# Router product on un-normalised rows, a reordered output projection, and an earlier start for three regions of the weight ring

## The chip, the cores and the metric

The kernel runs on one core of a Trainium2 chip. The core has five engines that matter here: TensorE (PE), VectorE (DVE), ScalarE (ACT), GpSimd (POOL) and SyncE (SP), whose queue issues the transfers from HBM. The metric is the device time of one execution in microseconds; the median of three runs of the kernel before is 1281.34 us (1281.11 to 1286.21).

## The reference, in short

One block of 256 tokens by 1024 channels, in fp32:

```python
u = _modulate(x, sh1, sc1)                      # layer norm, scale and shift
mix = _mixer(u, w_in, ...)                      # attention, gated linear attention, merge, w_out
x = _post_norm(ALPHA * x + (1 + g1) * mix, ln1_g, ln1_b)
u = _modulate(x, sh2, sc2)
ffn = _moe(u, w_router, b_router, w_up, b_up, w_down, b_down)
x = _post_norm(ALPHA * x + (1 + g2) * ffn, ln2_g, ln2_b)
```

The mixer projects u by w_in to 8 heads of forgetting attention, 4 heads of gated linear attention (GLA) and two gates. Each branch goes through a weight of its own, the two are merged by sigmoid gates, and w_out (1024 by 1024) projects the sum. `_moe` takes 32 logits per token from the normalised and modulated rows, keeps the four largest, takes a softmax over them, and adds up the outputs of those four experts, each a clamped SwiGLU with w_up (1024 by 2048) and w_down (1024 by 1024).

## The kernel before

The kernel is written as tasks, Python generators, that issue instructions to the five engines. The main line issues TensorE's large products, and between them `Tasks.tick` (line 346) lets the small tasks (GLA, attention, the vector work of the norms) put in theirs. When a task's turn comes is decided while the program is built, by a model of time, `Pace`: `Pace.cost` (line 95) gives each instruction a cost, and a task that yields a time waits until the modelled PE has come that far. The order on each engine is thus fixed in the program. All instructions pass through one helper, so every row has line 209, and rows are told apart by their tiles.

Weights stream from HBM through `Ring` (line 224). It holds regions of 1 MB by name; GV and KB, U1 and U2, LQ and FA, GS and GX are mates that lie side by side, shown as one tile of 2 MB (GVKB, U1U, LQFA, GSGX). A load is issued on SP's queue as soon as the program has a free region for it, in the order in which loads were asked for, and SP waits there until the last reader of that region is done. What stands behind it in SP's queue waits too.

The stages are these. The modulation vector and the input projection come first, with attention and GLA woven in (0 to about 304 us together with the branch products). Weights of the projections are split into two parts that TensorE multiplies in three passes: `split` (line 675) copies the high part on ACT and subtracts on DVE or POOL. The splits go into buffers of the pool `pair`: once GLA is done (`after_gla`, line 1329) the regions named in PAIR join it. `ada_task` (line 875) makes the columns of the modulation vector, `gate_mul` (line 1464) multiplies a branch by its gate and writes QA, and `merge` (line 1469) adds the branches. Then follow the output projection, eight half-loads of w_out (slots j) by two token blocks, in the order of the table ORDER, into the banks pz; `z_task` (line 1576) for each token block (z = alpha x + gated mixer output, layer norm, its transposes, the router product by `wr`, which `router_task` folds the modulation into, the four largest, one-hot rows W); and the gather, in which TensorE multiplies one-hot rows with the normalised rows (QA at that time). The loop over experts then runs `up_proj`, the activation and `down` for 32 experts, eight MB of w_up and four of w_down each. HALVES at the top gives the loads of the first experts as single regions.

In the tile names below, W_72, W_73, W_2713 are buffers of one pool; b_63 to b_70 are PSUM banks; x in rows of the order counts equal instructions in a row.

## Time and profile before

| | |
|---|---|
| median of three runs | 1281.34 us |
| profiled execution | 1283.55 us |
| its span | 1281.4 us |
| PE busy | 1177.7 us (92%) |
| DVE, ACT, POOL busy | 488.5, 262.0, 90.9 us |
| read from HBM | 469.43 MB, 367 GB/s over the span |

The table by stage below has one line for each stretch of the span. Its columns are the stretch, its length, the busy time and the instructions of PE, of PE's weight loads, of DVE, ACT and POOL, then the granted clock of TensorE as a share of full speed, the DMA share and the rate in GB/s. In the timelines each row is a group of neighbouring instructions of one kind: start in us, busy time, engine, line, operation, output<-input, shapes, count, and in brackets the idle time ahead of it with what ended it. SPq rows are issues of transfers, and their time includes waiting for the region.

### The profile page before, as it was taken

The numbers are of one execution on the slowest core, as the hardware profiler recorded it, in microseconds if no ns is written. First come the engines' busy times: TensorE is split into PE (matmuls) and PEld (weight loads), VectorE is DVE, ScalarE is ACT, GpSimd is POOL, SyncE is SP. The second block draws the span as 40 slices with busy tenths as digits, with TensorE's granted clock in tenths as the row PEclk, the third lists the DMA queues.
The fourth block names the chain that finished last, engine by engine and source line by source line (L and its number), as shares of the span: only waits on it lengthen the run. The fifth ranks groups of instructions, "written<-read, shape, count | busy, mean of one in ns | idle before, by whom it ended". The sixth has DMA issues, their size and how long they took to land. (4 is left out here: it accounts for less than half of the span.)

```text
span 1281.4 us, 15734 instructions
## 1 busy us (share of the span) xinstructions
PE 1177.7 (92%) x6478; PEld 603.9 (47%) x6478; DVE 488.5 (38%) x1053; ACT 262.0 (20%) x518; POOL 90.9 (7%) x61
## 2 busy tenths in 40 slices
PE   6999999989699999999989899898989898988995
PEld 4797677788534344343433334242434333333432
DVE  5645764457523224323333222322232332322233
ACT  3355544452211111010110101010101011010101
POOL 3412421020100000000000000000000000000000
PEclk9999999999799999999999999999999999999998
DMA  9953446895899999999999999999999999999994
GB/s 306 313 168 119 179 140 247 329 327 198 338 377 429 420 430 426 430 427 426 430 426 427 429 427 429 427 426 430 427 427 429 427 428 428 425 429 428 428 412 156
DMA packets 73061, 471.55 MB, mean 368 GB/s; under 512 B 7581, under 2 KB 28093, under 8 KB 45978
## 3 DMA queue, kind: packets, MB, share of 16 engines
q1 hardware_dynamic: 72794, 470.23, 90.2%
q8 instruction: 53, 0.87, 0.3%
q10 hardware_dynamic: 192, 0.27, 0.1%
q14 instruction: 22, 0.18, 0.0%
HBM read 469.43 MB, written 1.05 MB: 367 GB/s over the span
## 5 line engine op out<-in xcount | busy, mean ns | idle before, releaser
L209 PE MATMUL b<-U1U,W 128*128 128x256 f32 (+1 forms) x840 | 142.6, 410 | 11.0 <-DMA U1U<-in_w_down_dram 8.7
L209 DVE COPY W<-b 128x512 f32<-128x512 f32 x32 | 22.1, 691 | 296.8 <-PE b L209 296.8
L209 PEld LDWEIGHTS b<-U1U,W 128*128 128x128 f32 (+1 forms) x840 | 86.7, 169 | 67.1 <-issue 58.7
L209 DVE TENSOR_TENSOR W<-b,SP 128x512 f32<-128x512 f32 (+1 forms) x33 | 22.3, 675 | 221.1 <-PE b L209 221.1
L209 DVE TENSOR_TENSOR GL<-b,GL 128x512 f32<-128x512 f32 x124 | 76.9, 682 | 53.8 <-PE b L209 53.8
L209 PE MATMUL b<-YB1NB,W 128*64 128x512 f32 (+2 forms) x416 | 86.2, 542 | 4.5 <-DVE SP L209 4.0
L209 PE MATMUL b<-YAW,W 128*64 128x512 f32 (+1 forms) x384 | 82.3, 555 | 6.3 <-DVE SP L209 5.3
L209 PE MATMUL b<-R2YB,W 128*64 128x512 f32 x344 | 78.2, 595 | 9.1 <-DMA R2YB<-in_w_down_dram 7.2
L209 PE MATMUL b<-GSGX,W 128*64 128x512 f32 x336 | 76.2, 594 | 11.0 <-DMA GSGX<-in_w_down_dram 8.6
L209 PE MATMUL b<-R0R,W 128*64 128x512 f32 (+1 forms) x368 | 80.2, 578 | 4.6 <-DMA R0R<-in_w_up_dram 4.1
L209 PE MATMUL b<-GVKB,W 128*64 128x512 f32 x336 | 78.1, 608 | 5.0 <-DMA GVKB<-in_w_up_dram 5.0
L209 PE MATMUL b<-LQFA,W 128*64 128x512 f32 x336 | 77.8, 606 | 4.1 <-DMA LQFA<-in_w_up_dram 4.1
L209 ACT ACTIVATE W<-b 128x512 f32<-128x512 f32 x32 | 19.1, 597 | 303.3 <-PE b L209 303.3
L209 PE MATMUL b<-ADAM,W 128*64 128x512 f32 x336 | 75.9, 593 | 4.2 <-DVE SP L209 4.0
L209 ACT ACTIVATE SP<-b 128x256 f32<-128x256 f32 (+1 forms) x34 | 12.8, 378 | 309.3 <-PE b L209 309.3
L209 PEld LDWEIGHTS b<-W,QA 128*128 128x128 f32 x512 | 63.9, 203 | 13.9 <-DVE GL L209 11.4
L209 POOL TENSOR_TENSOR GL<-GL,QB 128x512 f32<-128x512 f32 x2 | 2.9, 1427 | 942.8 <-ACT GL L209 942.7
L209 PE MATMUL b<-W,QA 128*128 128x128 f32 x512 | 67.3, 291 | 0.6 <-DVE W L209 0.6
L209 PE MATMUL b<-W,SP 64*128 64x512 f32 (+1 forms) x264 | 63.9, 602 | 0.5 <-DVE W L209 0.5
L209 ACT ACTIVATE W<-b,scol 128x128 f32<-128x128 f32 x124 | 46.9, 457 | 64.4 <-PE b L209 60.0
L209 PEld LDWEIGHTS b<-YB1NB,W 128*64 128x64 f32 (+1 forms) x416 | 32.8, 143 | 55.4 <-issue 46.0
L209 PEld LDWEIGHTS b<-YAW,W 128*64 128x64 f32 (+1 forms) x384 | 30.8, 144 | 55.1 <-issue 44.6
(329 smaller groups left out, 1400.2 us busy)
## 6 DMA issues: line engine op xcount, KB each, us to landing
GVKB<-in_w_up_dram SPq DMA_DIRECT2D x21, 2048.0 KB
R0R<-in_w_up_dram SPq DMA_DIRECT2D x20, 2048.0 KB
LQFA<-in_w_up_dram SPq DMA_DIRECT2D x20, 2048.0 KB
YB1NB<-in_w_up_dram SPq DMA_DIRECT2D x11, 2048.0 KB
U1U<-in_w_up_dram SPq DMA_DIRECT2D x11, 2048.0 KB
YAW<-in_w_up_dram SPq DMA_DIRECT2D x11, 2048.0 KB
GSGX<-in_w_up_dram SPq DMA_DIRECT2D x11, 2048.0 KB
YAW<-in_w_down_dram SPq DMA_DIRECT2D x10, 2048.0 KB
```

What stands on the lines that cost most here:

```text
L209: r = f(*a, **k)
```

## The change

The layer norm behind the output projection is taken out of the router product. With r the inverse deviation and m the mean of a row, the normalised row is r (z - m) g + b, and the product with the router weights is linear in z: `weigh` folds g and b into the weights (two matmuls with a matrix of ones), keeps the constant row in `c1row`, and the raw z is transposed and multiplied at once by a new task, `zT_task`. `z_task` applies r, c1row, and the second norm's inverse deviation to the 32 logits. For token block 0 the sums for mean and variance come from accumulating outputs on DVE and a Square on ACT (`squares`), for block 1 from bn_stats as before. The normalising of block 0 leaves POOL. w_out is loaded by column halves, and ORDER runs the first column half for both token blocks, the second for block 0, then for block 1. PAIR keeps GV and KB; U1 and U2 go to the ring when GLA is done, and LQ is no longer called back. The count and gate matmuls go behind expert 0's up product. Two small loads of ln1's g and b as columns are new, and three constants of `Pace.cost` change, which moves the order of all tasks in the front.

```diff
-                return (n if n > m else 4 * m) / 2400.0 if a[1].dtype == F32R else n / 2400.0
+                return (n if n > m else 4 * m) / 2400.0 + 0.0135 if a[1].dtype == F32R else n / 1200.0
...
-                return n / 4200.0
+                return n / 2200.0
...
-        r = half_loads(w_out[0, (q // 2) * 512:], 4, (q % 2) * 512)[0]
+        r = half_loads(w_out[0, (q % 2) * 512:], 4, (q // 2) * 512)[0]
...
+    gbcol = small("gbcol", [128, 2, KC])
...
+        for i, r in enumerate((ln1_g, ln1_b)):
+            SP.dma_start(gbcol[:, i].rearrange("p (i j) -> p i j", j=UPJ),
+                         r[0].rearrange("(i p j) -> p i j", p=128, j=UPJ))
...
-            ring.recall(*ONCE)
+            ring.recall(*ONCE[:-1])
...
-    zx, ln1, ztb, late = [], [], [], []
+    both("U1")
+    ring.add("U1", "U2")
+    zx, ln1, late = [], [], []
...
-        DVE.tensor_tensor(tmp, wr, scol[:, 0, :, None].to_broadcast([128, KC, E]), op=OP.mult)
+
+        def weigh(shift, scale, row):
+            DVE.tensor_tensor(tmp, wr, shift[:, :, None].to_broadcast([128, KC, E]), op=OP.mult)
+            DVE.tensor_tensor(wr, wr, scale[:, :, None].to_broadcast([128, KC, E]), op=OP.mult)
+            yield
+            p = yield from aux.get()
+            for i, t in enumerate((tmp, wr)):
+                PE.matmul(p[:, i * 256:(i + 1) * 256], ones, t.rearrange(FLAT), start=True, stop=True)
+            yield
+            for i, d in enumerate((row, cs)):
+                DVE.tensor_reduce(d, p[:, i * 256:(i + 1) * 256].rearrange("p (k e) -> p e k", k=KC), axis=AX.X,
+                                  op=OP.add)
+            aux.put(p)
+            DVE.scalar_tensor_tensor(wr, cs[:, None, :].to_broadcast([128, KC, E]), -1.0 / D, wr,
+                                     op0=OP.mult, op1=OP.add)
...
+        yield from weigh(scol[:, 0], scol[:, 1], tmp[:, 0, :])
...
+        yield from weigh(gbcol[:, 1], gbcol[:, 0], c1row)
...
+
+    def zT_task(tb):
+
...
+            while f"z{tb}{n}" not in side.flags:
...
-        if tb:
-            ring.add("FA")
-        mv = mean_var(st)
-        end = pace.at["DVE"] + 0.15
-        u = u2[tb]
-        for n in range(2):
-            s = slice(n * 512, (n + 1) * 512)
-            yield end if n else pace.when(z[:, s]) - 0.85
+            yield pace.when(z[:, n * 512:(n + 1) * 512]) - 0.85
             p = yield from mm.get()
...
+            side.flags.add(f"zT{tb}{n}")
             ACT.activation(x1T[:, n * 4:n * 4 + 4, tb * 128:(tb + 1) * 128],
                            p.rearrange("p (a b) -> p a b", a=4), AF.Copy)
             mm.put(p)
...
+    def squares(z, tmp, sums):
+
+        mv = per.tile([128, 4], F32, tag="mv", bufs=6, name="mv")
+        DVE.tensor_scalar(mv[:, 0:1], sums[:, 0:1], sums[:, 1:2], 1.0 / D, op0=OP.add, op1=OP.mult)
+        DVE.tensor_scalar(sums[:, 2:3], mv[:, 0:1], -1.0, None, op0=OP.mult)
+        ACT.activation(tmp, z, AF.Square, bias=sums[:, 2:3], accum_out=sums[:, 3:4])
+        ACT.activation(mv[:, 1:2], sums[:, 3:4], AF.Copy, scale=1.0 / D)
+        return mv
...
+        for n in range(2):
+            while f"pz{tb}{n}" not in side.flags:
+                yield
+            s, zt = slice(n * 512, (n + 1) * 512), u[:, 0:512]
+            DVE.tensor_tensor(zt, pz[tb][n], g1row[:, s], op=OP.mult)
+            mm.put(pz[tb][n])
+            if tb:
+                DVE.scalar_tensor_tensor(z[:, s], z[:, s], ALPHA, zt, op0=OP.mult, op1=OP.add)
+                DVE.bn_stats(st[:, n, :], z[:, s])
+            else:
+                DVE.scalar_tensor_tensor(z[:, s], z[:, s], ALPHA, zt, op0=OP.mult, op1=OP.add,
+                                         accum_out=sums[:, n:n + 1])
+            side.flags.add(f"z{tb}{n}")
+            if n:
+                mv = mean_var(st) if tb else squares(z, u, sums)
+                rstd(mv)
+            yield
+        while not all(f"zT{tb}{n}" in side.flags for n in range(2)):
...
+        h = [z[:, i * 512:(i + 1) * 512] for i in range(2)]
+        if tb:
+            st = bn_tile()
+        DVE.scalar_tensor_tensor(h[0], h[0], mv[:, 0:1], ln1[0], op0=OP.subtract, op1=OP.mult)
+        DVE.scalar_tensor_tensor(mv[:, 3:4], mv[:, 0:1], -1.0, mv[:, 2:3], op0=OP.mult, op1=OP.mult)
+        if tb:
+            DVE.scalar_tensor_tensor(h[0], h[0], mv[:, 2:3], ln1[2], op0=OP.mult, op1=OP.add)
+        else:
+            sums = ss_tile()
+            DVE.scalar_tensor_tensor(h[0], h[0], mv[:, 2:3], ln1[2], op0=OP.mult, op1=OP.add, accum_out=sums[:, 0:1])
+        ACT.activation(h[1], h[1], AF.Identity, bias=mv[:, 3:4], scale=mv[:, 2:3])
+        yield
+        DVE.tensor_tensor(h[1], h[1], ln1[1], op=OP.mult)
+        if tb:
+            DVE.tensor_tensor(h[1], h[1], ln1[3], op=OP.add)
+            for n in range(2):
+                DVE.bn_stats(st[:, n, :], h[n])
+            ring.add("FA")
+            m1 = mean_var(st)
...
+            DVE.scalar_tensor_tensor(h[1], h[1], 1.0, ln1[3], op0=OP.mult, op1=OP.add, accum_out=sums[:, 1:2])
+        while f"raw{tb}" not in side.flags:
+            yield
+        if not tb:
+            m1 = squares(z, u, sums)
+        rstd(m1)
+        if not tb:
+            yield pace.at["ACT"] - 0.3
+        while f"raw{tb}" not in side.flags:
+            yield
+        p = V.raw[tb]
+        DVE.scalar_tensor_tensor(lg[:, 0:E], p[:, 256:256 + E], mv[:, 2:3], c1row, op0=OP.mult, op1=OP.add)
+        DVE.scalar_tensor_tensor(lg[:, 0:E], lg[:, 0:E], m1[:, 2:3], brow, op0=OP.mult, op1=OP.add)
+        mm.put(p)
         DVE.max(t8, lg[:, 0:E])
-        DVE.tensor_scalar(nm[:, 0:1], t8[:, 0:1], -1.0, None, op0=OP.mult)
         DVE.memset(t8[:, 4:8], NEG)
         DVE.match_replace(l2, t8, lg, TAKEN)
         DVE.tensor_tensor(msk[:, tb, :], l2[:, 0:E], lg[:, 0:E], op=OP.not_equal)
+        DVE.scalar_tensor_tensor(m1[:, 3:4], m1[:, 0:1], -1.0, m1[:, 2:3], op0=OP.mult, op1=OP.mult)
...
+        ACT.activation(u, z, AF.Identity, bias=m1[:, 3:4], scale=m1[:, 2:3])
...
+        yield pace.when(msk[:, tb, :]) - 0.85
...
-        s, n, k0 = NB_ + j, j // 2 % 2, j // 4 * 4 + j % 2 * 2
+        s, n, k0 = NB_ + j, j // 4, j % 4 * 2
         preps(s, AHEAD)
         mm_N([pz[0][n], pz[1][n]], parts[s], k0, m_of, KC, tbs)
         if 1 in tbs:
-            t = parts[s][2]
             used(s)
-            if s + AHEAD >= NO and Bufs.key(t) in where:
-                pair.free.remove(t)
-                ring.add(where[Bufs.key(t)])
+            if s == NO - 1 or NO - 1 in parts:
+                for t in [t for t in pair.free if Bufs.key(t) in where]:
+                    pair.free.remove(t)
+                    ring.add(where[Bufs.key(t)])
...
-    for tb in range(2):
-        PE.matmul(cnt[0:1, 0:E], onesb[:, 0:1], msk[:, tb, :], start=(tb == 0), stop=(tb == 1))
...
-    for tb in range(2):
-        for n in range(2):
-            PE.matmul(gt_p[64 * n:64 * n + E, tb * 128:(tb + 1) * 128], gates[:, tb, :], ident, start=True, stop=True)
...
+                PE.matmul(cnt[0:1, 0:E], onesb[:, 0:1], msk[:, tb, :], start=(tb == 0), stop=(tb == 1))
+                for n in range(2):
+                    PE.matmul(gt_p[64 * n:64 * n + E, tb * 128:(tb + 1) * 128], gates[:, tb, :], ident,
+                              start=True, stop=True)
...
-ORDER = [(T0, 0), (T0, 1), (T0, 2), (T0, 3), (T1, 0), (T1, 1), (T0, 4), (T0, 5), (T0, 6), (T0, 7),
-         (T1, 4), (T1, 5), (T1, 2), (T1, 3), (T1, 6), (T1, 7)]
+ORDER = [((0, 1), j) for j in range(4)] + [(T0, j) for j in range(4, 8)] + [(T1, j) for j in range(4, 8)]
...
-PAIR = ("U1", "U2", "GV", "KB")
+PAIR = ("GV", "KB")
```

The instructions on DVE around the first branch's gate product (QA<-QA,b_63). Rows with a weight region, W_.., YAW_.., GVKB or U1U_71 as output and the same tile as input are the subtraction of a split. Before:

```order
L209 TENSOR_TENSOR U1U_71<-LQFA,U1U_71 128x1024 x2
L209 TENSOR_TENSOR GVKB<-LQFA,GVKB 128x1024
L209 TENSOR_TENSOR GVKB<-R2YB_103,GVKB 128x1024
L209 TENSOR_TENSOR W_73<-R2YB_103,W_73 128x1024
L209 TENSOR_TENSOR YAW_606<-R2YB_103,YAW_606 128x1024
L209 TENSOR_TENSOR QA<-QA,b_63 128x512
L209 TENSOR_TENSOR QA<-QA,b_64 128x512
```

and after:

```order
L209 TENSOR_TENSOR W_72<-R0R_107,W_72 128x1024
L209 TENSOR_TENSOR GVKB<-R0R_107,GVKB 128x1024
L209 TENSOR_TENSOR GVKB<-ADAM,GVKB 128x1024
L209 TENSOR_TENSOR W_73<-ADAM,W_73 128x1024
L209 TENSOR_TENSOR YAW_607<-R2YB_103,YAW_607 128x1024
L209 TENSOR_TENSOR QA<-QA,b_63 128x512
L209 TENSOR_TENSOR QA<-QA,b_64 128x512
```

U1U_71 no longer takes splits, and the splits between the last branch weights and the gate product are other ones, from R0R_107 and ADAM.

The transfers that SP issues behind the ada columns (in_w_ada) into GSGX, whose region GLA frees. Before, from there on:

```order
L209 DMA R2YB_103<-in_w_in_dram 128x4x512
L209 DMA R0R_107<-in_w_in_dram 128x4x512
L209 DMA GSGX<-in_w_ada_dram 128x2048 x2
L209 DMA GL<-in_w_branch_a_dram 128x4x512
L209 DMA LQFA<-in_w_branch_a_dram 128x4x512
L209 DMA LQFA<-in_w_branch_b_dram 128x4x512
```

and after:

```order
L209 DMA ADAM<-in_w_in_dram 128x4x512
L209 DMA R2YB_103<-in_w_in_dram 128x4x512
L209 DMA GSGX<-in_w_ada_dram 128x2048 x2
L209 DMA GL<-in_w_in_dram 128x4x512
L209 DMA LQFA<-in_w_in_dram 128x4x512
L209 DMA LQFA<-in_w_ada_dram 128x2048
L209 DMA R2YB_103<-in_w_ada_dram 128x2048
L209 DMA R0R_107<-in_w_branch_a_dram 128x4x512 x2
```

Two loads of w_in now stand behind the two into GSGX, in GL and LQFA; all of w_in stood ahead of them before.

TensorE from the last rounds of the output projection (GSGX as the right operand) on. Transposes are products of ident and GL, the router product is QB with wr, the product with stack sums its partial results, the gather is W with QA. Before:

```order
L209 MATMUL b_66<-U1U_71,GSGX 128x512 x6
L209 MATMUL b_66<-GVKB,GSGX 128x512 x6
L209 MATMUL b_63<-ident,GL 128x128 x4
L209 MATMUL b_64<-ident,GL 128x128 x4
L209 MATMUL b_65<-QB,wr 32x128 x8
L209 MATMUL b_65<-stack,SP 128x32
L209 MATMUL b_66<-ident,GL 128x128 x4
L209 MATMUL b_63<-ident,GL 128x128 x4
L209 LDWEIGHTS strict
L209 MATMUL b_64<-msk,strict 128x32
L209 MATMUL b_66<-QB,wr 32x128 x8
L209 MATMUL b_67<-W_2713,QA 128x128 x4
```

and after:

```order
L209 MATMUL b_63<-ident,GL 128x128 x4
L209 MATMUL b_64<-GVKB,GSGX 128x512 x6
L209 MATMUL b_65<-ident,GL 128x128 x4
L209 MATMUL b_66<-YAW_607,GSGX 128x512 x6
L209 MATMUL b_66<-W_72,GSGX 128x512 x3
L209 MATMUL b_63<-ident,GL 128x128 x4
L209 MATMUL b_66<-W_72,GSGX 128x512 x3
L209 MATMUL b_66<-GVKB,GSGX 128x512 x12
L209 MATMUL b_64<-QB,wr 32x128 x8
L209 MATMUL b_65<-ident,GL 128x128 x4
L209 MATMUL b_64<-stack,SP 128x32
L209 MATMUL b_63<-QB,wr 32x128 x8
```

Three of the four groups of transposes moved into the output projection, and both router products now stand ahead of the first mask's product with strict.

## Rows read from the trace of the kernel before

**Rows 1.** By stage: the columns named above, core 0.
```profile
222.00:258.60 36.60, 34.63 (x272) 28.51 (x271) 14.14 (x16) 15.55 (x19) 4.09 (x2) 0.95 0.91 337
258.60:304.50 45.90, 41.62 (x310) 38.99 (x309) 29.44 (x38) 22.16 (x26) 9.45 (x5) 0.96 0.68 240
304.50:326.50 22.00, 22.00 (x98) 17.89 (x97) 12.99 (x20) 5.29 (x8) 2.50 (x4) 1.00 0.65 233
326.50:351.80 25.30, 15.40 (x98) 11.03 (x97) 15.45 (x48) 6.80 (x19) 4.18 (x3) 0.66 0.97 408
351.80:375.80 24.00, 23.09 (x102) 8.30 (x102) 7.97 (x21) 4.53 (x7) 0.00 (x0) 0.93 0.96 390
375.80:1243.00 867.20, 807.92 (x3950) 325.98 (x3948) 267.03 (x633) 100.12 (x244) 0.00 (x0) 1.00 1.01 427
```

**Rows 2.** Timeline of SP's queue.
```profile
217.43 1.15 SPq L209 DMA_DIRECT2D R0R<-in_w_in_dram  x2
...
238.74 0.97 SPq L209 DMA_DIRECT2D GSGX<-in_w_ada_dram  x2
...
328.31 8.18 SPq L209 DMA_DIRECT2D LQFA<-in_w_up_dram  x2
...
375.78 0.33 SPq L209 DMA_DIRECT2D GVKB<-in_w_up_dram  x1
```

**Rows 3.** PE's timeline in expert 0, and stretches of 1.7 us.
```profile
370.39 5.35 PE L209 MATMUL b<-GVKB,W 128*64 128x512 f32 x16
375.57 3.60 PE L209 MATMUL b<-YAW,W 128*64 128x512 f32 x16
...
341.80:343.50 1.70, 1.70 (x11) 1.70 (x11) 0.00 (x0) 0.00 (x0) 0.00 (x0) 0.59 1.02 434
370.70:372.40 1.70, 1.70 (x6) 0.49 (x4) 1.70 (x4) 0.00 (x0) 0.00 (x0) 0.50 1.02 434
374.10:375.80 1.70, 1.70 (x10) 0.58 (x8) 1.60 (x5) 0.42 (x1) 0.00 (x0) 1.00 0.36 154
```

**Rows 4.** PE's timeline in the last part of the input projection.
```profile
225.91 0.51 PE L209 MATMUL b<-U1U,YAW 128*128 128x256 f32 x2 [1.22 <-ACT YAW L209]
...
231.26 1.10 PE L209 MATMUL b<-ident,LQFA 128*128 128x128 f32 x8
...
240.10 3.04 PE L209 MATMUL b<-U1U,YAW 128*128 128x256 f32 x24
```

**Rows 5.** DVE and PE in the branch stage.
```profile
270.66 3.38 DVE L209 TENSOR_TENSOR YAW<-R2YB,YAW 128x1024 fp32r<-128x1024 f32 x1
...
274.79 1.49 PE L209 MATMUL b<-YB1NB,U1U 128*128 128x256 f32 x6 [3.89 <-DVE QA L209]
...
287.61 0.59 PE L209 MATMUL b<-gT,ones 128*128 128x256 f32 x2
```

**Rows 6.** PE, a group of four transposes in the branch stage.
```profile
278.21 0.69 PE L209 MATMUL b<-ident,ADAM 128*128 128x128 f32 x4
```

**Rows 7.** Timeline of all engines from there to expert 0.
```profile
301.81 1.06 ACT L209 ACTIVATE U1U<-R2YB 128x1024 fp32r<-128x1024 f32 x1
...
325.10 5.66 POOL L209 TENSOR_TENSOR GL<-GL,LQFA 128x512 f32<-128x512 f32 x4 [19.42 <-issue]
326.54 0.69 DVE L209 TENSOR_TENSOR LQFA<-b,ADAM 128x512 f32<-128x512 f32 x1 [2.43 <-PE b L209]
...
333.05 3.05 DVE L209 SCALAR_TENSOR_TENSOR GL<-GL,mv,LQFA 128x512 f32<-128x512 f32 x4
...
340.50 3.34 PE L209 MATMUL b<-W,QA 128*128 128x128 f32 x16
...
344.03 0.25 DVE L209 SCALAR_TENSOR_TENSOR lg<-b,mv,brow 128x32 f32<-128x32 f32 x1 [3.21 <-PE b L209]
...
346.07 3.38 PE L209 MATMUL b<-W,QA 128*128 128x128 f32 x16 [0.60 <-DVE W L209]
...
351.47 0.41 PE L209 MATMUL b<-ident,gates 128*32 128x128 f32 x4 [1.43 <-DVE gates L209]
```

More of the change, by code (lines that the diff above doesn't have):

```diff
@@ L1389, in again_task @@
             SP.dma_start(t, rows(r, D))
-        while ring.busy("LQ"):
-            yield
-        own("LQ")
-        ztb.extend(cut("LQ", 512, 0, 2))
         side.flags.add("again")
@@ L1560, in slots_out @@
                 DVE.tensor_scalar(d, q, scol[:, 1, k:k + 1], scol[:, 0, k:k + 1], op0=OP.mult, op1=OP.add)
[L1562 to L1565 removed]
+    V.raw = {}
+    def zT_task(tb):
+        z = zx[tb]
         for n in range(2):
[L1567 to L1609 removed]
+            while f"z{tb}{n}" not in side.flags:
+                yield
+            yield pace.when(z[:, n * 512:(n + 1) * 512]) - 0.85
             p = yield from mm.get()
@@ L1633, in z_task, with ss_tile @@
         PE.matmul(p[:, 256:256 + E], lT, stack, start=True, stop=True)
-        yield
+        V.raw[tb] = p
+        side.flags.add(f"raw{tb}")
+    def ss_tile():
+        return per.tile([128, 6], F32, tag="ss", bufs=3, name="ss")
+    def squares(z, tmp, sums):
[5 more added lines that the diff above has]
+        return mv
+    def z_task(tb):
+        while not ("g1" in side.flags and "again" in side.flags):
+            yield
+        z, u, st, sums = zx[tb], u2[tb], bn_tile(), ss_tile()
         lg, l2, ex = [small(f"{n}{tb}", [128, E + 4]) for n in ("lg", "l2", "ex")]
@@ L1637, in z_task @@
         DVE.memset(lg[:, E:E + 4], NEG)
-        DVE.scalar_tensor_tensor(lg[:, 0:E], p[:, 256:256 + E], mv[:, 2:3], brow, op0=OP.mult, op1=OP.add)
+        for n in range(2):
[15 more added lines that the diff above has]
+            yield
@@ L1659, in z_task @@
                 px.append((yield from aux.get()))
-            yield pace.when(u[:, 512 * i:512 * i + 512]) - 0.8
+            yield pace.when(u) - 0.8
             while tb and f"half{i}" not in side.flags:
@@ L1668, in z_task @@
                 aux.put(px[i])
+        side.flags.add(f"placed{tb}")
         DVE.scalar_tensor_tensor(ex[:, 0:E], ex[:, 0:E], 1.0, msk[:, tb, :], op0=OP.mult, op1=OP.mult,
@@ L1677, in block_kernel @@
     side.add(z_task(1))
+    side.add(zT_task(0), "again")
+    side.add(zT_task(1), "again")
     order = ORDER
     for tbs, j in order:
[L1680 removed]
+        s, n, k0 = NB_ + j, j // 4, j % 4 * 2
         preps(s, AHEAD)
@@ L1706, in block_kernel @@
     gT = small("gT", [128, T])
-    for tb in range(2):
-        for n in range(2):
-            PE.matmul(gt_p[64 * n:64 * n + E, tb * 128:(tb + 1) * 128], gates[:, tb, :], ident, start=True, stop=True)
     ACT.preload_act_table(AF.Sigmoid)
@@ L1976, in block_kernel @@
             for tb in range(2):
+                PE.matmul(cnt[0:1, 0:E], onesb[:, 0:1], msk[:, tb, :], start=(tb == 0), stop=(tb == 1))
+                for n in range(2):
+                    PE.matmul(gt_p[64 * n:64 * n + E, tb * 128:(tb + 1) * 128], gates[:, tb, :], ident,
+                              start=True, stop=True)
+            for tb in range(2):
                 ACT.activation(zx[tb], zx[tb], AF.Copy, scale=ALPHA)
```

62 lines of the change are left out of this document (8 added, 54 removed).

## The prediction

> **What bounds the kernel now.** I read the busy time by stage first, then what SP issues where two stages meet, then the stages' operations in order of time. From 375.8 to 1243 us the weight transfer is full: DMA share 1.01, 427 GB/s, while TensorE is busy 808 of 867 us [rows 1]. Nothing in the diff changes the bytes or the loop over experts, so that stretch can only shift. What decides when it starts is one queue entry: SP issues the load into region GVKB at 375.78 [rows 2], when TensorE has read expert 0's weights out of it (sixteen matmuls from 370.39, 5.35 us [rows 3]). In 374.1 to 375.8 the DMA share is 0.36: the early loads have run out and the transfers wait for this issue [rows 3]. So at this point the kernel waits for TensorE, not for memory. TensorE starts expert 0 at 351.8 and GVKB is free 24.0 later, so the end of the run stands at a fixed distance behind the start of the experts, T = 351.8, as long as the early loads last. The stages before T are TensorE's: 34.63 busy of 36.60, 41.62 of 45.90, 22.00 of 22.00 [rows 1]. Only the last, 326.5 to 351.8, is a chain across engines: TensorE is busy 15.40 of 25.30 with a granted clock of 0.66 [rows 1]. I therefore add up what each part does to T. Letters: I is the end of the input projection (258.6), S and E the start and end of the output projection (304.5, 326.5); a prime marks the new time.
>
> **Input projection, to I.** TensorE is idle for 36.60 − 34.63 = 1.97 us here, of which 1.22 stand ahead of 225.91, for a split weight [rows 4]; its load was issued at 217.43 [rows 2], because no region was free sooner. After, GLA's last transposes stand some 15 us of TensorE work earlier in the order, so GSGX, GL and LQFA come free earlier and take loads. I take half, −1.0; ends −2.0 (all of it) and, if the new order makes stalls of its own, the +6 of the last rival.
>
> **Branches, I to S.** The 45.9 hold 4.3 of idle. The large piece is 3.89 ahead of 274.79: TensorE waits for DVE's product of gate and branch [rows 5]. That product stood behind weight splits on DVE, one of them 3.38 us long at 270.66 [rows 5]. PAIR now holds two regions, not four, so five buffers are free for splits, not seven, and DVE runs fewer of them ahead: after, the product is done about 11.1 us behind I', and the bank is wanted 13.6 behind it. Cost of the same stage: the second call of weigh adds two matmuls over wr and gT; the pair before takes 0.59 [rows 5], so with the second operand's pair about +1.0 in all. −4.3 + 1.0 = −3.3. Ends: −4.3 (the pair lies in a gap) and +1.0 (another split blocks the product). The two column loads of gbcol go out near 80 us, where DMA is mostly idle; I cost them at nothing.
>
> **Output projection, S to E.** The twelve rounds keep their matmuls: 22.0. Three of the four groups of z's transposes now lie inside, four matmuls each, 0.69 by the row at 278.21 [rows 6]: +2.1. Both token blocks go together for the first four column-halves, so block 0's first half is complete early and its transposes and its normalising lie beside the last rounds. The splits that come later because of two buffers fewer have 2 to 3 us of slack by my walk through the order, so no stall is added. Ends 0 and +4 (one late split).
>
> **Tail, E to T, 25.3 before.** What goes: POOL's four passes over block 0, 5.66 us from 325.10, for which TensorE's transposes waited [rows 7]; and the count and gate matmuls ahead of T, 349.4 to 351.8, 2.3 us, their last waiting 1.43 for the gates [rows 7]. They move behind expert 0's up product. What comes, in time behind E', at the durations of the same forms: z's last half by 1.5 (0.69 each, as at 326.54 [rows 7]), its statistics by 2.45; on DVE, second half of block 0 normalised by 3.95, first of block 1 by 5.55, second by 7.4 (four such passes took 3.05 at 333.05 [rows 7]), statistics by 9.0. Block 0's logits to mask take 1.4 more, 10.45 (the like chain before begins at 344.03 and its one-hot releases the gather at 346.07 [rows 7]), small ones 10.75. Then ACT normalises block 0 for the gather, 1.06 for 128x1024 [rows 7], and the inverse deviation of block 1 is queued behind that: 12.6. Block 1's mask 13.8, block 0's one-hot 14.65. Block 0's gather is sixteen matmuls; the two before took 3.34 and 3.38 [rows 7], at a granted clock of 0.59 in the row that I have for the first [rows 3]. TensorE waits before it, as it did then, so 3.4: 18.1. Block 1's follows with no break: 1.7 if the clock is up by then, 3.4 if not; between, and closer to the first, since in the down product the clock rose from 0.50 to 1.00 while TensorE worked on [rows 3]: T' = E' + 20.2. 20.2 − 25.3 = −5.1. Ends: 18.0 (both gathers at 1.7) and 25.3.
>
> The Trainium skill ("TensorE: Matmul & The Clock Gate", section on why it matters for your kernels) says that idle gaps between bursts of matmuls drop the engine to half rate. The wait of several us ahead of the gathers is such a gap, and the trace agrees: 0.50 to 0.59 behind waits. If that speaks for both gathers, T' is E' + 21.4; I hold it as a case.
>
> **Behind T.** The count and gate matmuls and their copies, about 2.3 at the rate of before, less the wait: +0.5, since expert 0 waits for the activation there anyway. Ends −1.75 (the sixteen matmuls of 370.39 took 5.35 at clock 0.50, those of 375.57 3.60 [rows 3]; if TensorE stops less, the difference is won) and +1.0.
>
> **Whether transfers last.** Before, two loads into LQFA at 328.31 held SP's queue for 8.18 us, waiting on their region [rows 2]. After, U1U and LQFA take 3 MB before E', 7.3 us at 427 GB/s, in a stretch whose DMA share is 0.65 to 0.68 [rows 1]. From E' about 9 MB, 22 us, are left; they are done near S' + 65, GVKB's issue on TensorE's path is due at S' + 24.05 + 20.2 + 24.5 = S' + 68.7. TensorE's path still decides, by 3.6. Without the 3 MB the transfer would end near S' + 72.4 and take its place.
>
> **Sum.** −1.0 − 3.3 + 2.1 − 5.1 + 0.5 = −6.8 against the profiled execution's 1283.55 (its span is 1281.4): 1276.75. That execution lies 2.2 above the median of the runs, 1281.34; the same distance gives 1274.5.
>
> **Rivals.**
> - *More is won.* The clock stays up into expert 0 (−1.75 − 0.5), both gathers run at it (−2.2), the whole front idle goes (−1.0): 1274.5 − 5 or so, 1269.5. For it: clock 0.95 and 0.96 in the two stages before S [rows 1], which shorter gaps could raise as well; another 3 at most, so 1266. Against: the wait ahead of the gathers stays.
> - *Both gathers cold.* +1.2: 1275.7.
> - *The transfer takes over.* The 3 MB do not come ahead of E', because the splits of the last weights hold U1U, or GLA's rows hold LQFA. Then the issue is worth nothing past S' + 72.4, 3.7 late: 1278.2. For it: the DMA share is already 0.97 in the tail [rows 1]. Against: the order has the LQFA load six entries ahead of GVKB's.
> - *The queue blocks the input projection, and it is not faster or is slower.* The last two loads of w_in now go to GL and LQFA and stand on SP behind two ada loads into GSGX, which wait for GLA's end (238.74 before [rows 2]). GSGX twice and GL are 3 MB, 7.4 us, and from issue to the first bytes 1.7 (375.78 to 377.5). Their first matmuls are wanted four rounds of 3.04 [rows 4] and an ada pair of 1.9 ahead of I' = 257.6, at 243.5, two more for the split. So each us by which GLA ends past 232.5 costs one. At 239.3, half a us later than before, the gain is gone: 1281.3; slower by 0.5% needs 245.8. For it: the loads behind are in order and nothing can pass. Against: the order puts the last transposes of GLA 41.6 us of TensorE work ahead of I', against 26.2 before (231.26 [rows 4]), which makes its end about 223. GLA is a chain of small operations across DVE and ACT, so that order is a wish and not a time.
>
> **How the numbers follow.** Forecast 0.45, with its own range 1272 to 1278; more is won 0.22; cold gathers 0.08; transfer 0.13; queue 0.12. A difference under 0.5%, 6.4 us, is what a measurement of this kernel can't well tell from none, so faster means under 1274.9. That splits the forecast's case: 0.25 faster, 0.20 same. Faster 0.25 + 0.22 = 0.47; slower 0.10 of the queue's 0.12; the rest same, 0.43. The range runs from the lower end of what can be won, 1266, to 1284, which takes in the transfer and the start of the queue's case and leaves out the rest.
>
> **What would show it.** In the profile after: a stage from I' to S' near 42.6 with no wait over 1 us for QA; an output projection near 24 us; E' to the first expert matmul near 20, with POOL absent; the DMA share falling for a moment ahead of GVKB's issue, about 24.5 behind T'. It would be wrong if TensorE waits in the input projection for GL or LQFA, if GVKB's issue is long past before the transfers ahead of it end, or if the wait for the two masks in the tail is as long as before.

## The result and the profile after

The changed kernel takes 1269.02 us (median of 4 runs, 1266.06 to 1270.11) against 1283.78 (4 runs) before: a ratio of 0.9881, interval 0.9849 to 0.9914. The forecast was 1274.5, and faster. By the profiled executions it is 1283.55 to 1269.44, the spans 1281.4 to 1267.6, so 13.8 us of span to account for. The stages after, in the columns of [rows 1], cut where the work changes over:

```profile
222.00:254.70 32.70, 32.70 (x272) 27.99 (x272) 14.05 (x13) 14.24 (x16) 0.00 (x0) 1.00 1.03 391
254.70:295.25 40.55, 40.55 (x314) 38.20 (x313) 32.60 (x44) 19.24 (x22) 4.96 (x3) 1.00 0.81 295
295.25:318.60 23.35, 23.35 (x110) 19.31 (x108) 14.37 (x26) 9.39 (x15) 2.68 (x1) 1.00 0.64 256
318.60:338.30 19.70, 9.46 (x76) 8.21 (x75) 12.15 (x44) 7.71 (x18) 0.00 (x0) 0.65 0.95 385
338.30:360.60 22.30, 21.73 (x111) 8.19 (x112) 8.02 (x24) 5.94 (x10) 0.00 (x0) 1.00 1.00 410
360.60:1226.20 865.60, 806.64 (x3940) 325.68 (x3938) 269.01 (x637) 100.52 (x245) 0.00 (x0) 1.00 1.01 426
```

The reader is to see two things beside the shorter stages: TensorE has no idle time from 222 to 318.6, and the granted clock is 1.00 in the three stages where it was 0.95, 0.96 and 0.93 in [rows 1]. Against the terms of the prediction:

| | before | after | difference | forecast |
|---|---|---|---|---|
| end of the input projection, I | 258.6 | 254.7 | −3.9 | −1.0 |
| branches, I to S | 46.0 | 40.6 | −5.4 | −3.3 |
| output projection, S to E | 21.95 | 23.45 | +1.5 | +2.1 |
| tail, E to T | 25.3 | 19.6 | −5.7 | −5.1 |
| expert 0, T to GVKB's issue | 24.0 | 22.3 | −1.7 | +0.5 |
| sum, GVKB's issue | 375.78 | 360.60 | −15.2 | −6.8 |

SP's queue after, as in [rows 2]:

```profile
219.82 1.80 SPq L209 DMA_DIRECT2D GSGX<-in_w_ada_dram  x2
221.66 0.44 SPq L209 DMA_DIRECT2D GL<-in_w_in_dram  x1
...
303.06 0.33 SPq L209 DMA_DIRECT2D U1U<-in_w_up_dram  x1
...
360.60 0.33 SPq L209 DMA_DIRECT2D GVKB<-in_w_up_dram  x1
```

GLA gave GSGX free at 219.8, 12.7 us ahead of the point from which the queue would have cost something, so the last loads of w_in were in time. U1U's load is issued at 303.1, 15.6 us ahead of the output projection's end, where it was 1.3 ahead before (325.17). The transfers around GVKB's issue at 360.6, in stretches of 2 us and two shorter ones:

```profile
358.00:360.00 2.00, 2.00 (x12) 0.62 (x10) 1.93 (x6) 0.42 (x1) 0.00 (x0) 1.00 0.97 410
360.00:360.50 0.50, 0.50 (x6) 0.21 (x4) 0.40 (x2) 0.00 (x0) 0.00 (x0) 1.00 0.93 360
360.50:361.50 1.00, 1.00 (x8) 0.32 (x6) 0.90 (x3) 0.00 (x0) 0.00 (x0) 1.00 0.16 66
360.00:362.00 2.00, 2.00 (x12) 0.68 (x10) 1.79 (x6) 0.11 (x1) 0.00 (x0) 1.00 0.83 229
362.00:364.00 2.00, 2.00 (x12) 0.72 (x10) 1.28 (x4) 0.31 (x1) 0.00 (x0) 1.00 0.70 262
364.00:366.00 2.00, 2.00 (x12) 0.61 (x10) 0.00 (x0) 0.00 (x0) 0.00 (x0) 1.00 0.99 401
```

They still run dry, though for less time than before: against 427 GB/s the rates from 360 to 366 leave 0.9 + 0.8 + 0.1 = 1.8 us unused, and 374 to 380 in the kernel before leave 2.8. So TensorE's path decided, as the prediction had it, but with less to spare than it worked out. Its 3.6 us run from the end of the early loads to GVKB's issue. The loads ended where it put them, near 360.3 or S′ + 65, and the issue came 3.4 us earlier than summed, so that some 0.3 of the 3.6 was left. The rest of the 1.8 lies behind the issue, until the transfers are at full rate again.

Of the 15.2 us at GVKB's issue 13.8 are left at the end. SP's issues stay 15.17 to 15.18 ahead up to the eleventh after GVKB and are 13.73 ahead from the twelfth on, into LQFA, which waits for TensorE in expert 2. There TensorE waits 1.11 us in both kernels. Before, with the clock in the 4 us behind the wait:

```profile
425.33 3.72 PE L209 MATMUL b<-SP,ones 1*128 1x512 f32 x8 [1.11 <-DVE GL L209]
428.00:432.00 4.00, 4.00 (x11) 1.03 (x11) 1.87 (x5) 1.71 (x4) 0.00 (x0) 0.57 1.00 426
```

and after, with 8 us:

```profile
410.17 4.47 PE L209 MATMUL b<-SP,ones 1*128 1x512 f32 x8 [1.11 <-DVE GL L209]
412.80:416.80 4.00, 4.00 (x10) 1.04 (x10) 1.12 (x3) 1.50 (x3) 0.00 (x0) 0.50 1.00 426
416.80:420.80 4.00, 4.00 (x16) 1.19 (x14) 1.94 (x6) 0.42 (x1) 0.00 (x0) 0.74 1.00 426
```

The same wait is followed by more time at half clock. The change has no edit there, and no run shows why the clock differs.

### The profile page after: what moved, and what is told of

Read it like the earlier page. It is cut to its first block, busy times and chain, and to the rows that moved or that the text cites. A ratio compares the mean times of both kernels' runs of the same rounds, so it can differ in the third digit from the quotient of the medians.

```text
span 1267.6 us, 15762 instructions
## 1 busy us (share of the span) xinstructions
PE 1170.3 (92%) x6482; PEld 601.1 (47%) x6482; DVE 494.6 (39%) x1070; ACT 265.5 (21%) x525; POOL 73.2 (6%) x53
## 5 line engine op out<-in xcount | busy, mean ns | idle before, releaser
L209 DVE TENSOR_TENSOR W<-b,SP 128x512 f32<-128x512 f32 (+1 forms) x33 | 22.3, 676 | 221.3 <-PE b L209 221.3
L209 PE MATMUL b<-YB1NB,W 128*64 128x512 f32 (+2 forms) x440 | 89.4, 528 | 5.7 <-DVE SP L209 4.0
L209 PEld LDWEIGHTS b<-YB1NB,W 128*64 128x64 f32 (+1 forms) x440 | 35.7, 146 | 56.4 <-issue 45.0
```

What stands on the lines that cost most here:

```text
L209: r = f(*a, **k)
```

## The experiments

In all of them the stages are read from the traces: I, S, E and T as in the prediction. An execution's whole front can lie 1.8 us earlier or later with the same instructions (last section), so lengths of stages are compared, and ratios to the kernel before on the same chip, not medians.

**The cost constants alone, taken back and put in.**

```diff
-                return (n if n > m else 4 * m) / 2400.0 + 0.0135 if a[1].dtype == F32R else n / 1200.0
+                return (n if n > m else 4 * m) / 2400.0 if a[1].dtype == F32R else n / 2400.0
-                return n / 2200.0
+                return n / 4200.0
```

> The changed kernel with the three old constants of the cost model. In the changed kernel the input projection ends at 254.68 us, 3.9 earlier than before, and the branch stage takes 40.6 instead of 45.9. My theory: the constants set the order in the front, and that order alone took away TensorE's wait of 2 us near 226 and, with it, a stretch at half the clock. Then the projection ends near 258.5 again with a granted clock near 0.95 in its last 36 us, the branch stage stays between 40.6 and 44 since PAIR still holds two regions, and the run is 4 to 7 us slower than the changed kernel, near 1274. Rival: the earlier release of regions did it; then the projection ends near 254.7 and the time stays near 1269.

Measured: ratio 0.9934 (0.9909 to 0.9959). I is 258.48 again, and the last 36.6 us of the input projection are those of [rows 1]:

```profile
221.88:258.48 36.60, 34.68 (x272) 28.57 (x271) 14.13 (x16) 15.53 (x19) 4.05 (x2) 0.95 0.91 339
```

The branch stage stays at 41.25, output projection and tail at 23.5 and 18.8. So the constants carry 3.8 of the 3.9 of the first term. GVKB's issue is at 364.30, 3.7 later than in the changed kernel. The other way round, the reversed edit in the kernel before:

> The kernel before with nothing but the three new constants. Theory (order alone): the input projection ends near 254.7 without a wait over 0.5 us; the branch stage keeps a wait of 3 to 4 us for the gate product, as nine splits still stand ahead of it; tail and expert 0 as before (25.3 and 24.0). Total about 4 us less than before, near 1279.5. Rival (sooner regions): the projection ends at 258.6 as before and the time does not move, 1283.

Measured: ratio 0.9958 (0.9932 to 0.9983). I comes at 252.85 without a wait. This execution's front is one of those that lie 1.8 earlier, so 3.9 of the 5.7 us are the edit's. Tail and expert 0 take 25.4 and 25.1. The branch stage keeps a wait, of 2.56 instead of 3.89, with the clock at 1.00 behind it, and takes 42.5 instead of 46.0, which was not expected. The theory holds in both directions; the rival, that released regions did it, is out.

**The four regions of PAIR.**

```diff
-    both("U1")
-    ring.add("U1", "U2")
...
-PAIR = ("GV", "KB")
+PAIR = ("U1", "U2", "GV", "KB")
```

> The changed kernel with the four regions in PAIR and U1 and U2 not joining the ring when GLA ends. The input projection ends near 254.7 in any case. Theory of the prediction (splits ahead of the gate product on DVE make the wait): the branch stage takes 43 to 46 us, with a wait of 2 to 4 us for QA and a granted clock under 1.00 behind it; 1272 to 1274. Rival (the front's new order is enough): the branch stage stays at 40.6, and only the early load into U1U comes later, so that the time moves by less than 2 us.

Measured: ratio 0.9921 (0.9897 to 0.9945). The wait for the gate product is back, and the branch stage takes 43.39, 2.8 longer:

```profile
269.77 3.10 PE L209 MATMUL b<-YB1NB,U1U 128*128 128x256 f32 x24 [2.56 <-DVE QA L209]
254.56:297.95 43.39, 40.83 (x314) 38.31 (x313) 34.82 (x44) 21.15 (x24) 9.80 (x5) 1.00 0.71 252
```

Splits ahead of the gate product make this wait, as the prediction had it. The new constants alone leave the same 2.56 of the 3.89 us before, and the two regions alone, with the old constants, leave none of them: there the longest wait of the stage is 0.40, and the clock 1.00. One part of the expectation fails: behind these 2.56 us the clock stays at 1.00. U1U's load is issued at 320.12, not 303.06, and the DMA share is 0.96 to 1.04 from 356 to 364, around GVKB's issue at 363.50: without U1U's early 2 MB the transfers have no slack left, even with TensorE 2.9 us later.

**The router product on normalised rows again.**

```diff
-            while f"z{tb}{n}" not in side.flags:
+            while f"h{tb}{n}" not in side.flags:
...
+        side.flags.add(f"h{tb}0")
...
+            side.flags.add("h11")
...
-        yield from weigh(gbcol[:, 1], gbcol[:, 0], c1row)
...
-        DVE.scalar_tensor_tensor(lg[:, 0:E], p[:, 256:256 + E], mv[:, 2:3], c1row, op0=OP.mult, op1=OP.add)
-        DVE.scalar_tensor_tensor(lg[:, 0:E], lg[:, 0:E], m1[:, 2:3], brow, op0=OP.mult, op1=OP.add)
+        DVE.scalar_tensor_tensor(lg[:, 0:E], p[:, 256:256 + E], m1[:, 2:3], brow, op0=OP.mult, op1=OP.add)
```

> The changed kernel with the router product taken on the normalised rows again: z's transposes wait for the first norm, the second call of weigh goes, and the logits need one operation. All else stays (two sets of sums, loads, order, the place of the gates). Theory: the output projection is about 1.4 us shorter, the transposes and the product go back behind the norm, and the tail takes 24 to 25 us against 19.7; expert 0 starts 3 to 4 us later, the run is 2 to 4 us slower, near 1272. Rival: the norm on DVE bounds the tail in both forms, so expert 0 starts within 1 us of the changed kernel's and the time does not move.

Measured: ratio 0.9869 (0.9846 to 0.9893), expert 0 at 338.54 against 338.33. My theory falls, and the rival's outcome is what came. The tail is 2.6 us longer (22.2), but the output projection is 1.5 shorter without the transposes (21.96) and the branch stage 0.8 without the second call of weigh (39.74). So the masks come at the same time to within 0.14 us. In the changed kernel:

```profile
326.77 0.21 DVE L209 BATCH_NORM_AGGREGATE mv<-bn 128x2 f32<-128x12 f32 x1
328.38 0.19 PE L209 MATMUL b<-msk,strict 128*128 128x32 bf16 x1 [1.26 <-DVE msk L209]
```

and in this run:

```profile
324.34 0.21 DVE L209 BATCH_NORM_AGGREGATE mv<-bn 128x2 f32<-128x12 f32 x1
327.34 0.25 DVE L209 SCALAR_TENSOR_TENSOR lg<-b,mv,brow 128x32 f32<-128x32 f32 x1 [2.53 <-ACT mv L209]
328.52 0.18 PE L209 MATMUL b<-msk,strict 128*128 128x32 bf16 x1 [0.36 <-DVE msk L209]
331.72 0.19 PE L209 MATMUL b<-msk,strict 128*128 128x32 bf16 x1 [2.98 <-DVE msk L209]
```

The rival's reason is not what the rows show: DVE is through with the statistics 2.4 us sooner here, and then waits 2.53 us for ACT, which makes block 0's second deviation in 325.3 to 327.3. The product on raw rows, the part that the change is named after, shortens the tail by 2.6 us, costs 2.3 in the two stages ahead of it, and is worth 0.2 us at expert 0.

**The count and gate matmuls back ahead of expert 0.**

```diff
+    for tb in range(2):
+        PE.matmul(cnt[0:1, 0:E], onesb[:, 0:1], msk[:, tb, :], start=(tb == 0), stop=(tb == 1))
+    for tb in range(2):
+        for n in range(2):
+            PE.matmul(gt_p[64 * n:64 * n + E, tb * 128:(tb + 1) * 128], gates[:, tb, :], ident, start=True, stop=True)
     ACT.preload_act_table(AF.Sigmoid)
...
-                PE.matmul(cnt[0:1, 0:E], onesb[:, 0:1], msk[:, tb, :], start=(tb == 0), stop=(tb == 1))
-                for n in range(2):
-                    PE.matmul(gt_p[64 * n:64 * n + E, tb * 128:(tb + 1) * 128], gates[:, tb, :], ident,
-                              start=True, stop=True)
...
```

> The changed kernel with the count and gate matmuls back ahead of expert 0's up product. In the kernel before they held TensorE from 349.4 to 351.8, 2.3 us. Theory: expert 0 starts 1.0 to 2.3 us later than the 338.3 of the changed kernel (less than 2.3 since the first of the gates are ready by 333.2), the 0.6 us they take behind the up product go, and GVKB's issue comes 0.5 to 1.7 us after 360.6; the time moves by about 1 us, which the runs can hardly tell. Rival: they delay nothing, as they lie in a wait for the gathered rows; expert 0 starts at 338.3.

Measured: E to T is 22.25, 2.6 more than in the changed kernel, and GVKB's issue 363.16, also 2.6 later; ratio 0.9881 (0.9864 to 0.9899), which does not tell it from the changed kernel. TensorE waits 2.00 us for the gates:

```profile
340.55 0.41 PE L209 MATMUL b<-ident,gates 128*32 128x128 f32 x4 [2.00 <-DVE gates L209]
...
357.18 0.44 PE L209 MATMUL b<-ident,SP 128*128 128x128 f32 x2 [0.79 <-DVE gT L209]
340.89:363.16 22.27, 21.37 (x102) 7.87 (x102) 6.36 (x17) 4.11 (x6) 0.00 (x0) 1.00 0.92 360
```

Behind the up product they cost nothing at all, since T to GVKB's issue is 22.27 with and without them. So this move is 2.6 of the tail's 5.7.

Taken back one at a time, four parts of the change thus cost at GVKB's issue 3.7 us (constants), 2.9 (regions), 2.6 (count and gate matmuls) and 0.2 (raw rows), 9.4 of the 15.2 together. The new order of w_out and the new division of the norm between DVE, ACT and POOL were not taken back alone, so what they are worth is not shown.

**A wait, and the same place filled.** No part of the computation uses what these two add.

```diff
+        if s == NW - 12:
+            sc = small("gT", [128, T])
+            POOL.eng.tensor_tensor(sc, wr.rearrange(FLAT), wr.rearrange(FLAT), op=OP.add)
+        if s == NW - 11:
+            d = aux.now()
+            PE.eng.matmul(d[0:64, 0:256], ident[:, 0:64], sc, start=True, stop=True)
+            for _ in range(3):
+                POOL.eng.tensor_tensor(sc, wr.rearrange(FLAT), wr.rearrange(FLAT), op=OP.add)
+            PE.eng.matmul(d[0:64, 0:256], ident[:, 0:64], sc, start=True, stop=True)
+            aux.put(d)
```

The other run has eighteen such products in this place, and no additions on GpSimd.

> The changed kernel with a wait put into TensorE's stream eleven weight rounds ahead of the end of the input projection: a small product that reads a tile, three 128x256 additions on GpSimd that overwrite it, and a second small product that reads it. No other instruction moves; the results of the added work are not used. TensorE waits about 2 us. Theory (a wait on TensorE costs its length and then a stretch at half clock): the input projection ends 3.5 to 4.5 us later than 254.7, with a granted clock near 0.95 in its last 36 us and at 0.50 right behind the wait. Rival (a wait costs its length): it ends 2.0 to 2.5 us later and the clock stays at 1.00.

> The changed kernel with 18 products of 64x256 in the same place, into a bank that nothing reads, and no wait. At the 0.11 us that such a shape takes at full clock they hold the stream up for 2.0 us. Both theories: the input projection ends 2.0 us later than 254.7, with the clock at 1.00; it is the other half of the run with a wait, so that the two differ in the clock alone.

Measured, with the wait (ratio 0.9913, 0.9896 to 0.9931), TensorE's rows and two stretches behind it:

```profile
216.73 0.65 PE L1359 MATMUL b<-gT,ident 128*64 128x256 f32 x2
220.36 1.12 PE L1362 MATMUL b<-gT,ident 128*64 128x256 f32 x2 [2.99 <-POOL gT L1361]
221.41 4.07 PE L209 MATMUL b<-U1U,YAW 128*128 128x256 f32 x24
220.00:222.00 2.00, 1.64 (x4) 0.88 (x5) 0.00 (x0) 0.00 (x0) 0.31 (x1) 0.53 1.09 401
222.00:224.00 2.00, 2.00 (x13) 2.00 (x13) 0.00 (x0) 0.00 (x0) 0.00 (x0) 0.62 0.98 328
```

and filled (ratio 0.9917, 0.9900 to 0.9933):

```profile
215.28 7.98 PE L1357 MATMUL b<-wr,ident 128*64 128x256 f32 x36
223.20 3.13 PE L209 MATMUL b<-U1U,YAW 128*128 128x256 f32 x24
224.47:261.07 36.60, 36.60 (x305) 31.89 (x303) 14.13 (x13) 14.33 (x16) 0.00 (x0) 1.00 0.88 336
```

My size for the products was wrong by four: each is two instructions of 0.22 us, and the 18 took 8.0 us. The front of the filled run also lies 1.5 us earlier, so the two ends (260.21 and 261.07) can't be compared as meant. The stretch behind them can: from the start of the YAW round to I it is 37.78 in the changed kernel (216.90 to 254.68), 37.87 behind the products and 38.80 behind the wait. The wait itself was 2.99, and the instructions behind it lost 1.0 in that stretch and 0.47 in the small product ahead of it (1.12 against 0.65). So a wait of 3.0 us on TensorE cost 4.5. That is the theory, with the clock at 0.53 and 0.62 behind the wait, and at 1.00 where the place was filled with work.

**One-hot rows of block 0 first.** In the changed kernel's tail ACT has block 0's rows (QA) ready at 329.74, and TensorE waits to 332.3:

```profile
328.50 1.24 ACT L209 ACTIVATE QA<-GL,mv 128x1024 f32<-128x1024 f32 x1 [2.06 <-DVE nm L209]
...
330.40 0.25 DVE L209 SCALAR_TENSOR_TENSOR lg<-lg,mv,brow 128x32 f32<-128x32 f32 x1 [1.78 <-ACT mv L209]
...
331.58 0.19 PE L209 MATMUL b<-msk,strict 128*128 128x32 bf16 x1 [2.99 <-DVE msk L209]
...
332.30 6.11 PE L209 MATMUL b<-W,QA 128*128 128x128 f32 x32 [0.53 <-DVE rk L209]
```

DVE stands 1.78 us for block 1's inverse deviation, which ACT makes behind block 0's rows, and block 0's rank stands behind that.

```diff
             m1 = mean_var(st)
+            rstd(m1)
...
-        while f"raw{tb}" not in side.flags:
+        while f"raw{tb}" not in side.flags or tb and "hot0" not in side.flags:
...
         group_onehots(0, tb)
+        side.flags.add(f"hot{tb}")
```

> The changed kernel with block 0's rank and one-hot rows put ahead of block 1's logits on DVE, and block 1's inverse deviation ahead of block 0's normalising for the gather on ACT. In the changed kernel TensorE waits 2.99 us for block 1's mask and 0.53 more before the first gather at 332.3. Theory: the gather starts near 329.8, when ACT has normalised block 0, and expert 0 near 336.0, 2.3 us earlier; GVKB's issue near 358.3. Of that the early loads give about 1.8 (that much transfer time was idle around 360 to 366), so later issues come 1.5 to 2.3 us earlier, the time near 1267. Rival: the first gather waits for ACT all the same and block 1's mask only comes later behind it, so that expert 0 starts within 0.7 us of 338.3.

Measured: ratio 0.9838 (0.9822 to 0.9854). E to T is 17.48, 2.1 less than the changed kernel's 19.62, by the mechanism named: the first gather starts 11.0 behind E and not 13.6. GVKB's issue is at 356.69, and from 356 to 362 the transfers leave 0.7 us unused where the changed kernel left 1.8. The median was 1265.48 against 1285.94 before on that chip. It beats the kernel before for certain; its interval and that of the changed kernel still overlap. Of the profiled execution's lower time 1.8 us are an earlier front, which is not the edit's.

**Products in the tail's waits.** These add work that nothing uses.

```diff
+    def fill(n):
+        d = aux.now()
+        for _ in range(n):
+            PE.eng.matmul(d[0:64, 0:256], ident[:, 0:64], wr.rearrange(FLAT), start=True, stop=True)
+        aux.put(d)
...
+        if tb:
+            fill(7)
...
```

> The changed kernel with 7, 3 and 6 products of 64x256 put where TensorE waits in the tail (behind block 1's router product, behind its row sums, behind block 0's rank), into a bank that nothing reads; by the run with 18 of them one takes 0.44 us. They end before what TensorE waits for. Theory: the clock stays at 1.00 up to the gathers, whose 32 matmuls take 3.3 to 3.8 us instead of 6.11; expert 0 starts 16.8 to 17.4 behind the end of the output projection instead of 19.6, and the run is about 2 us faster than the changed kernel (ratio to the kernel before near 0.986). Rival: the gathers run slowly for another reason (their shape, weight loads that each take as long as the matmul), and take 6 us all the same; then the time does not move.

Measured: ratio 0.9861 (0.9837 to 0.9885), E to T 19.09, only 0.5 less:

```profile
321.97 0.63 PE L209 MATMUL b<-stack,SP 128*128 128x32 f32 x2 [0.95 <-ACT SP L209]
322.53 1.08 PE L209 MATMUL b<-QB,wr 128*32 128x128 f32 x16
323.55 5.73 PE L1578 MATMUL b<-wr,ident 128*64 128x256 f32 x14
...
333.91 4.01 PE L209 MATMUL b<-W,QA 128*128 128x128 f32 x32
```

The gathers do take 4.0 instead of 6.1, but the clock was already down when the filling began (16 small products took 1.08, in the changed kernel 0.64), so its first 14 instructions took 5.7 and not 3.1, and the gathers start 1.6 us late. The clock theory holds; as a gain it nearly cancels itself.

**Both, and the order of the last weights.** The same products (11 and 2) on the run with the earlier one-hot rows; then, without them, block 1's last rounds in the order 6, 7, 4, 5, which frees GV and KB sooner (the marks of the first and last product of a sum move with it); then all three.

```diff
-ORDER = [((0, 1), j) for j in range(4)] + [(T0, j) for j in range(4, 8)] + [(T1, j) for j in range(4, 8)]
+ORDER = [((0, 1), j) for j in range(4)] + [(T0, j) for j in range(4, 8)] + [(T1, j) for j in (6, 7, 4, 5)]
```

> The run with the earlier one-hot rows, with 11 and 2 such products where TensorE still waits there. Theory: the first gather takes 1.7 us instead of 3.67, the second starts as soon as ACT has normalised block 1, and expert 0 starts near 15.8 behind the output projection instead of 17.5. But in the run without the products the early loads lasted almost to GVKB's issue (DMA share 0.94 behind it), so of these 1.7 us at most 0.5 are seen: the DMA share stays at 1.00 around GVKB's issue, and the time is that of the run with the earlier one-hot rows (ratio near 0.984). Rival: TensorE's path is still what counts; then the ratio is near 0.9825 and a dip of the DMA share is seen.

> The run with the earlier one-hot rows, and block 1's second column half in the output projection in the order 6, 7, 4, 5, so that the two weights that sit in GV and KB are done two rounds sooner. GVKB's first load is issued 2.9 us ahead of the end of the output projection instead of 0.1 behind it, in a stretch in which the transfers were idle for some 7 us. Theory: expert 0 starts at the same 17.5 behind; the early loads end about 3 us sooner, and the transfers are idle for about 3 us ahead of GVKB's second load, so that this alone wins nothing (ratio near 0.984). Rival: the transfer already binds; then the time falls by up to 1 us more.

> Earlier one-hot rows, products in the waits, and the order 6, 7, 4, 5 together. Theory: expert 0 starts near 15.8 behind the output projection, GVKB's second issue 22.3 later, and since the early loads now end 3 us sooner the gain reaches the end: about 1.5 us less than with the earlier one-hot rows alone, a ratio near 0.9825. Rival: if the two single steps each win nothing because something else binds, this one wins nothing either (0.984).

Measured: ratios 0.9858 (0.9834 to 0.9883), 0.9863 (0.9839 to 0.9887) and 0.9863 (0.9839 to 0.9887); E to T 17.30, 17.33 and 18.76. In the first, each gather runs at speed, but the clock falls half a us into the filling (0.50 in 324 to 326), which ends late:

```profile
323.02 6.65 PE L1578 MATMUL b<-wr,ident 128*64 128x256 f32 x22
...
330.97 2.13 PE L209 MATMUL b<-W,QA 128*128 128x128 f32 x16
...
334.12 2.15 PE L209 MATMUL b<-W,QA 128*128 128x128 f32 x16 [0.98 <-ACT QA L209]
```

The transfers have no slack left there, as expected: the DMA share is 0.99 to 1.02 from 356 to 362, around GVKB's issue at 358.47. In the second, GVKB's first load is issued 2.7 us ahead of E, and the transfers wait again for its second, at 356.60:

```profile
356.00:358.00 2.00, 2.00 (x12) 0.69 (x10) 1.79 (x6) 0.10 (x1) 0.00 (x0) 1.00 0.68 188
358.00:360.00 2.00, 2.00 (x12) 0.72 (x10) 1.28 (x4) 0.31 (x1) 0.00 (x0) 1.00 0.76 287
```

That is 1.8 us unused (3 were expected), with E to T 0.15 shorter and no gain in time. In the third the filling, for the most part at half clock, costs 1.4 us of tail, so it doesn't test what the two would win together; that stays open. None of the four is told apart from the run with the earlier one-hot rows alone.

## Why the prediction came out as it did

The direction, the bound and the place were right. The run's end moved with GVKB's issue, that moved with TensorE's path, and each stage moved to the side that was forecast except expert 0. The time, 1269.0, is in the range and 5.5 below the forecast: 15.2 us at GVKB's issue where 6.8 were summed. Three terms were mis-sized most, and all three for leaving out TensorE's time at half clock. The rival "more is won" had named that loss (the clock of 0.95 and 0.96, "another 3 at most"), outside the sum. That the time falls beside its 1269.5 is in part luck: the 1269.5 left those 3 us out and took in both gathers at full clock (−2.2), which did not come.

*Input projection, "I take half, −1.0".* It was −3.9. All of the 1.97 idle went, and with it the half clock behind it: 0.05 of 36.6 us is 1.8. Together 3.8. The clock of 0.95 stood in the row that I read, and the sum priced the idle time alone. Before, the clock behind this wait and behind the branch stage's was:

```profile
228.00:230.00 2.00, 2.00 (x10) 0.49 (x13) 1.71 (x3) 0.99 (x2) 0.00 (x0) 0.50 0.52 70
276.00:278.00 2.00, 2.00 (x12) 2.00 (x10) 2.00 (x4) 0.00 (x0) 0.00 (x0) 0.50 0.99 372
```

*Branches, "−4.3 + 1.0 = −3.3".* It was −5.4. The 0.96 of the branch stage over 46 us is another 1.8: −4.3 − 1.8 + 0.8 (the second call of weigh, by the run without it) is −5.3. That splits ahead of the gate product made the wait is shown by the run with four regions, which has it back at 2.56, and by the run with the old constants and two regions, which has none.

*Behind T, "+0.5".* It was −1.7. I kept the clock's loss in expert 0 (0.93 of 24 us, 1.7) as before, and cost the matmuls moved there at 0.5. They cost nothing, as the run with them put back shows. The loss did not lie at expert 0's start: its first eight matmuls took 1.94 us in both kernels, and the clock fell late, to 0.50 in 370.7 to 372.4 [rows 3], behind a wait of 0.79 for the activation. In the changed kernel that wait is 0.57 and the clock stays at 1.00. But it stays there in the run with the matmuls put back too, with the wait at 0.79 again, so why the loss went is open. The end of −1.75 that the text named was the right value, by a reason ("if TensorE stops less") that this run doesn't bear out.

So 5.3 of the 8.4 us that were missing are TensorE's time at half clock, 3.6 of them behind waits that the change removed. The run with a wait put in shows that cost directly, 1.5 us behind 3.0. The Trainium skill ("TensorE: Matmul & The Clock Gate", section on why it matters for your kernels) says that idle gaps between bursts of matmuls send the engine back to half rate. The rows agree for the wait put in (0.53 and 0.62 behind it); the waits of the input projection, 1.22 and 0.75, are shorter than the gaps that the page names, and the clock fell behind them all the same. I had applied the page to the tail alone, where it was the smaller matter. The loss is no fixed price: behind the 2.56 us wait of the run with four regions the clock stayed at 1.00.

*Tail, "−5.1".* It was −5.7, by other parts than the sum had. Both gathers ran slowly (6.11 us for the 32, near the 6.8 of the rival of cold gathers, where the sum had 5.5). The chain ahead of the first was shorter than summed, 13.6 for 14.7, and hardly shorter than before (340.50 − 326.5 = 14.0 [rows 7]). What the tail won lies behind that: the two gathers follow each other at once, 6.1 us from the first's start to the end of the second, where it was 9.0 before since the second waited for block 1's mask [rows 7], and the gate matmuls are gone from there. That the second mask comes in time for it is not the raw-row product's doing, as the run without it shows; the prediction did not ask which part brings it.

*Output projection, "+2.1".* +1.5: a group of four transposes takes 0.63 in its row but holds the stream up by some 0.4 to 0.5.

The rival of the queue did not come (GSGX issued at 219.8). The rival of the transfer did not come, with 0.3 of the 3.6 us that the sum gave it; the runs that shorten the tail further come up against it.

Three readings of the prediction were wrong without harm to the sum. The matmuls that read GVKB from 370.39 are the first of expert 1's up product, not expert 0's and not a down product; they still release that region. "9 MB, 22 us" behind E′ would end at S′ + 46 and not at S′ + 65: from E′ to GVKB's issue the transfers carried 16.7 MB (399 GB/s over 41.89 us). And the "1.7 from issue to the first bytes" was read off stretches of 1.7 us; in stretches of 0.25 a burst of 786 GB/s stands at 376.75, 1.0 behind the issue.

## What to carry to other kernels

Price a wait on TensorE at its length and at what the granted clock in the row behind it shows: a stage with idle time and a clock of 0.95 loses twice, and gives both back. A change with one name has several parts; here a cost model's constants, the released regions and the gate matmuls, each taken back alone, cost 3.7, 2.9 and 2.6 of the 15 us, and the router product on raw rows 0.2. When transfers are idle for under 2 us around the issue that restarts them, the next gain on the compute side needs earlier free regions first.

## What was not expected of the hardware

TensorE's first products run at one of two rates, with the same instructions. In the changed kernel:

```profile
15.59 1.95 PE L209 MATMUL b<-ident,GL 128*128 128x128 f32 x8
```

and in the run with the earlier one-hot rows, which has the same instructions there:

```profile
15.13 1.07 PE L209 MATMUL b<-ident,GL 128*128 128x128 f32 x8
```

The column of the granted clock reads 1.00 there in both, so what sets the rate is not shown. Six of the fourteen profiled executions have the faster rows. In four of them the difference of 1.8 us is still there at the end of the input projection, 252.91 against 254.68 in these two kernels. In the other two, the changed kernel with products in the tail's waits and the run with all three steps, it is gone again, at 254.73 and 254.60: the clock falls to half near 97 us, in a stretch in which TensorE is never idle. In the first of them:

```profile
97.00:103.00 6.00, 6.00 (x28) 4.71 (x28) 2.14 (x6) 1.97 (x6) 0.00 (x0) 0.50 0.00 0
```

So a wait is not the only thing that a fall of the clock can follow, and half clock behind a wait need not be the wait's doing; what made it fall here is not shown. These 1.8 us are as large as most of the single steps that were tested here, and probably part of the spread of the runs of one kernel, of which one execution each was profiled.
